# Keeping only the low part of a split weight in DRAM, and casting its high part again in the second pass

## The chip, the cores and the metric

The kernel runs on one core of one Trainium2 chip. The metric is the device time of one execution in microseconds (us). TensorE (PE in the profile; PEld is its weight load), VectorE (DVE), ScalarE (ACT), GpSimd (POOL) and SyncE (SP) each run their own list of instructions in order and wait for one another by semaphores. All DMAs of this kernel are issued from SP's list, one after the other; SPq in the profile is that issuing.

## The reference

One step of a hybrid decoder layer over 1024 prompt tokens and 8 single sample tokens, width 1024, all in float32:

```python
p = jnp.einsum('btd,dn->btn', x, w_in)                    # 1024 -> 9360 columns
p_gla, p_rwkv, p_gate = _split(p, (GLA_COLS, RWKV_COLS, GATE_COLS))
...  # gated linear attention: 4 heads, chunked, with a state
...  # RWKV-7: 16 heads, a recurrence over the tokens, with a state
m = (jax.nn.sigmoid(gate_a) * jnp.einsum('btc,cd->btd', o_gla, w_up_gla)
     + jax.nn.sigmoid(gate_b) * jnp.einsum('btc,cd->btd', o_rwkv, w_up_rwkv))
out = jnp.einsum('btd,de->bte', m, w_out)
y_out = _layernorm(DEEPNORM_ALPHA * x + out, ln_g, ln_b, LN_EPS)
```

The outputs are `y_out` for both groups of tokens and their new states.

## The kernel before

**Two passes over the tokens.** The tokens are split into two tiles: the first 512 prompt tokens and the 8 samples (520 columns, worked on as pieces of 256 and 264), and the other 512 prompt tokens (one piece of 512). For each tile the whole input projection is done, 73 blocks of 128 output columns, and between its matmuls the scans of that tile (GLA heads, RWKV pairs with a triangular solver) are woven in. Only then come, for both tiles, the two up projections (8 blocks each per tile, "the up stage"), the output projection and the layer norm ("the last stage").

**Split weights.** TensorE's float32r matmul rounds its operands, so each weight and each x is held as two parts: `hi`, the value cast to float32r, and `lo`, the rest. A block of the projection is 8 steps over the depth, and each step is three matmuls: hi times x high, hi times x low, lo times x high. A block's weight comes in two halves of 512 columns. A half is loaded as `wraw` (128 x 512 float32, 256 KB, 3 buffers). ScalarE casts it into `wpart[:, 0]`, VectorE (or GpSimd) subtracts and writes `wpart[:, 1]` (128 x 2 x 512, 512 KB, 5 buffers). TensorE takes the halves in order from the list `self.ws`, and a `wpart` buffer is free again when its block's last piece is done.

**What the second pass does for its weights.** The weights of the two passes are the same. So in the first pass each finished half is also written to DRAM, both parts together (`kept`, a DRAM tile named `w<column>_<half>`, 512 KB), and in the second pass the half is loaded from there, both parts in one DMA, with no work on ScalarE or VectorE. The profile calls the write `w<-wpart` and the reload `wpart<-w`. This is `load_w`, with its streams `high` (the casts) and `low` (the subtractions and the writes). The up projections' weights come the first pass's way: load, cast, subtract.

**What sets the order.** Nothing is ordered by hand. Every piece of work is a generator (a stream), and `Order.run` holds all streams. At each turn it prices the next operation of each stream with its own table of costs and gaps, takes the one that can start earliest (less a priority of its kind), puts it at the end of its engine's list, and goes on. Any change of one operation can therefore change the order of everything behind it, on every engine. All instructions are recorded in helpers, so nearly all of them show line L219 in the profile: groups are told apart by tile names. Names that the text below uses: `proj`, `big`, `pch`, `pY` are PSUM banks (2, 4, 1, 1 of them); `xs` the split x; `row` general rows in SBUF; `wide`, `rh`, `bk`, `gg`, `XT`, `X`, `A`, `L`, `LD`, `XD` belong to the scans, and `XD`, `L`, `XT`, `X` to the solver, which sends its blocks through DRAM by 16 DMAs in a row (`XD<-X`, `L<-gg`, `XT<-XD`, `X<-XD`, four each).

`evacuate` empties the bank of a finished piece. `up_row` and `load_gates` merge the two branches in the up stage: the first branch's result goes to the DRAM tile `mg`, and `c.half` tells that it may be read back.

Of the kernel before, what the change touches and what calls it, by code (L numbers as in the profile page):

```python
# [10 lines left out]
F32 = mybir.dt.float32  # L11
# [9 lines left out]
P = 128  # L21
# [397 lines left out]
class Kern(Order):  # L419
# [224 lines left out]
    def load_w(self):  # L644

        H = NK // 2
        todo = [(b.src, b.c0, j, b.c.i) for b in self.plan if b.src is not None for j in range(2)]
        raws, his, los, kept = [], [], [], {}

        def high():  # L650
            n = 0
            while True:
                yield lambda: len(raws) > n
                w = yield from self.get("wpart")
                yield self.A.copy(w[:, 0], raws[n][0])
                his.append(w)
                n += 1
                if n == count:
                    return

        def low():
            for n in range(count):
                yield lambda: len(his) > n
                w = his[n]
                raw, src, c0, j, i = raws[n]
                yield self.E.tensor_sub(w[:, 1], raw, w[:, 0].bitcast(F32))
                self.free(raw)
                if src is self.a["w_in"] and i == 0:
                    kept[c0, j] = self.dr.tile([P, 2, 512], F32, name=f"w{c0}_{j}")
                    yield self.S.dma_start(kept[c0, j], w.bitcast(F32))  # L670
                self.ws.append(w)
                los.append(w)
            self.w_done = True
        count = sum(src is not self.a["w_in"] or i == 0 for src, _, _, i in todo)
        self.spawn(high(), "w")
        self.spawn(low(), "w")
        for n, (src, c0, j, i) in enumerate(todo):
            if src is self.a["w_in"] and i:
                yield lambda: len(los) == len(raws)
                w = yield from self.get("wpart")  # L680
                yield self.S.dma_start(w.bitcast(F32), kept[c0, j])
                self.ws.append(w)
                continue
            raw = yield from self.get("wraw")

            yield from self.load(f"w{n}", self.S.dma_start(raw, src[c0 // P, j]))
            raws.append((raw, src, c0, j, i))

    def blocks(self):
        xs = None  # L690
        for at, b in enumerate(self.plan):
            if b.swap is not None:
                self.spawn(self.load_x(*b.swap), "x")
            if xs is None:
                yield lambda: len(self.xq) > 0
                xs = self.xq.pop(0)
            if b.src is None:
                yield from b.act(xs)
                xs = None
# [4 lines left out]
            tiles = list(enumerate(b.c.tiles))  # L704
            for group in [tiles] if at == 0 else [[x] for x in tiles]:
                fin = group[-1][0] == len(tiles) - 1
                banks = []
                for _ in group:
                    banks.append((yield from (self.get("proj") if b.src is self.a["w_in"] else self.get_of("proj", "pY", "big"))))
                for k in range(NK):  # L710
                    yield lambda: len(xs) > k
                    if len(w) <= k // 4:
                        yield lambda: self.ws
                        w.append(self.ws.pop(0))
                    hi, lo = (w[k // 4][:, v, k % 4 * P:k % 4 * P + P] for v in range(2))
                    xh, xl = xs[k]
# [9 lines left out]
                self.spawn(self.evacuate(evac, group, banks, b.post if fin else None), "evacuate")  # L726
            if b.last:
                xs = None

    def evacuate(self, evac, group, banks, post):  # L730
        for (tt, (t0, n)), ps in zip(group, banks):
            yield from evac(tt, t0, n, ps[:, :n])
            self.free(ps)
        if post is not None:
            post()
# [742 lines left out]
    def load_gates(self):  # L1478

        yield lambda: self.projected  # L1480
        for c in self.ctx:
            for n in range(2):
                for x in range(NK):
                    gt = yield from self.row(c.n, SPARE_ROWS)
                    yield self.S.dma_start(gt, self.sg[c.i][n][x])
                    m = None
                    if n:
                        m = yield from self.row(c.n, SPARE_ROWS)
                        yield lambda: c.half > x
                        yield self.S.dma_start(m, self.mg[c.i][x])  # L1490
                    yield self.A.activation(gt, gt, AF.Sigmoid)
                    self.gts.append((gt, m))

    def up_row(self, c, n, x):
        turn = self.ups
        self.ups += 1
        yield lambda: len(self.gts) > turn

        def ev(tt, t0, w, q):
            gt, m = self.gts[turn]  # L1500
            s = slice(t0, t0 + w)
            yield self.V.tensor_mul(gt[:, s], q, gt[:, s])
            if n:
                yield self.E.tensor_add(gt[:, s], gt[:, s], m[:, s])
            if tt == len(c.tiles) - 1:
                yield self.S.dma_start(self.mg[c.i][x], gt)
                self.free(gt)
                c.half += 1
                if n:
                    self.free(m)  # L1510
                    c.merged += 1
        return ev
# [205 lines left out]
    def run_all(self):  # L1718
        self.chained, self.headed, self.decayed = -1, 0, 0
        self.first = ["wa", "x0", "w0", "x1", "x2", "x3", "w1", "x4", "x5", "x6", "x7", "pv", "shift", "w2", "w3", "cst"]  # L1720
        self.has = set()
        self.sampled = self.w_done = self.projected = False
        self.ups = 0
        self.plan, self.xq, self.ws, self.wo, self.gts, self.l2s = [], [], [], [], [], []
        self.setup()
        self.ctx = [SimpleNamespace(i=i, base=b, n=n, ns=ns, tiles=t, gla_done=0, rwkv_done=0, fronts=0, lw_ready=False,
                                    alr_ready=0, merged=0, half=0, gated=0,
                                    rg=[[] for _ in range(NPAIR)], gg=[[] for _ in range(GH)])
                    for i, (b, n, ns, t) in enumerate(PASS)]
# [67 lines left out]
```

## Time and profile before

| | us |
|---|---|
| median of 3 runs | 1497.9 (1496.89 to 1500.17) |
| the profiled execution | 1493.88 |
| its span, first to last instruction | 1492.1 |
| TensorE busy | 1466.4 |
| TensorE weight load busy | 1282.5 |
| VectorE busy | 1201.9 |
| ScalarE busy | 880.1 |
| GpSimd busy | 115.5 |

The profiled execution lies 4.0 us below the median of the timed runs, and 1.8 us of it are outside the span. The core moved 197.32 MB from HBM and 118.61 MB to it. The first pass takes the first 600 us of the span, about; the second pass goes to 1190, the up stage to about 1390, and the last stage to the end. Engine times in the profile are busy times of the engine; a busy TensorE counts pipelined matmuls whose ends are modelled, so its idle time alone does not tell how dense its work is.

### The profile page before, as it was taken

The numbers are of one execution on the slowest core, as the hardware profiler recorded it, in microseconds if no ns is written. First come the engines' busy times: TensorE is split into PE (matmuls) and PEld (weight loads), VectorE is DVE, ScalarE is ACT, GpSimd is POOL, SyncE is SP. The second block draws the span as 40 slices with busy tenths as digits, with TensorE's granted clock in tenths as the row PEclk, the third lists the DMA queues.
The fourth block names the chain that finished last, engine by engine and source line by source line (L and its number), as shares of the span: only waits on it lengthen the run. The fifth ranks groups of instructions, "written<-read, shape, count | busy, mean of one in ns | idle before, by whom it ended". The sixth has DMA issues, their size and how long they took to land.

```text
span 1492.1 us, 30560 instructions
## 1 busy us (share of the span) xinstructions
PE 1466.4 (98%) x10678; PEld 1282.5 (86%) x10678; DVE 1201.9 (81%) x3159; ACT 880.1 (59%) x2221; POOL 115.5 (8%) x217
## 2 busy tenths in 40 slices
PE   9999999999999999999999999999999999999997
PEld 6998999999999999787877887787788899988786
DVE  6697889988998898979887998888777876756665
ACT  6665767767677677565754556465646746644210
POOL 1001002101120002001001010101000000000000
PEclk9999999999999999999999999999999999999999
DMA  9876697668767877675566565656554768887432
GB/s 310 282 267 207 221 314 227 218 220 302 234 220 221 297 239 241 185 237 168 165 203 175 161 199 180 181 154 171 177 172 135 234 197 258 282 300 264 143 106 85
DMA packets 211253, 319.01 MB, mean 214 GB/s; under 512 B 91683, under 2 KB 107180, under 8 KB 211100
## 3 DMA queue, kind: packets, MB, share of 16 engines
q1 hardware_dynamic: 211100, 317.06, 66.6%
q8 instruction: 85, 1.39, 0.4%
q14 instruction: 68, 0.56, 0.1%
HBM read 197.32 MB, written 118.61 MB: 212 GB/s over the span
## 4 chain that ended last, share of the span: by engine, by line
PE 83%; DVE 7%; DMA 4%; ACT 2%; issue 1%; SPq 1%; POOL 0%; POOLq 0%; DVEq 0%; ACTq 0%
PE proj L219 51%; PE big L219 22%; PE pch L219 6%; PE pY L219 5%; DVE row L219 2%; SPq L219 1%; DMA row<-o_rwkv 1%; ACT row L219 1%; DMA wraw<-w_in 1%; DVE X L219 1%; DVE wpart L219 1%; DMA wide<-LD 1%; DMA row<-state_rwkv 1%; DVE Xt L219 0%; ACT L397 0%
## 5 line engine op out<-in xcount | busy, mean ns | idle before, releaser
L219 PE MATMUL proj<-xs,wpart 128*128 128x264 f32 (+2 forms) x5640 | 1028.6, 327 | 1.2 <-DVE row L219 0.8
L219 PEld LDWEIGHTS proj<-xs,wpart 128*128 128x128 f32 x5640 | 814.4, 189 | 80.8 <-issue 10.3
L219 ACT CAST wpart<-wraw 128x512 fp32r<-128x512 f32 x210 | 130.2, 623 | 84.1 <-PE big L219 31.0
L219 DVE TENSOR_TENSOR wpart<-wraw,wpart 128x512 fp32r<-128x512 f32 x205 | 142.5, 697 | 33.4 <-ACT wpart L219 30.2
L219 DVE TENSOR_TENSOR row<-row 128x512 f32<-128x512 f32 (+10 forms) x295 | 156.8, 536 | 10.9 <-DMA row<-state_rwkv 6.2
L219 ACT ACTIVATE row<-row 128x512 f32<-128x512 f32 (+4 forms) x229 | 138.6, 610 | 26.2 <-DVE row L219 13.8
L219 POOL TENSOR_TENSOR row<-row 128x256 f32<-128x256 f32 (+7 forms) x74 | 70.3, 955 | 669.5 <-DVE row L219 232.9
L219 DVE TENSOR_TENSOR Xt<-X,wide 128x60 f32<-128x60 f32 (+24 forms) x496 | 108.4, 218 | 15.4 <-DMA wide<-LD 2.7
L219 DVE TENSOR_TENSOR X<-X,Xt 128x60 f32<-128x60 f32 (+24 forms) x496 | 106.0, 214 | 12.0
L219 ACT ACTIVATE row<-proj,omu 128x256 f32<-128x256 f32 (+1 forms) x99 | 54.3, 549 | 72.2 <-PE proj L219 71.8
L219 PE MATMUL big<-xs,wpart 128*128 128x512 f32 (+2 forms) x552 | 93.5, 324 | 0.0
L219 PEld LDWEIGHTS big<-xs,wpart 128*128 128x128 f32 x552 | 81.1, 188 | 8.7
L219 PE MATMUL big<-row 128*128 128x128 f32 (+4 forms) x464 | 86.6, 317 | 0.3 <-DVE Xt L219 0.3
L397 ACT ACT_TABLE_LOAD x64 | 82.1, 1283 | 1.1
L219 DVE SCALAR_TENSOR_TENSOR wide<-pch,pc,s0p 64x64 f32<-64x64 f32 x208 | 58.5, 281 | 28.3 <-PE pch L219 23.9
L219 DVE SCALAR_TENSOR_TENSOR row<-proj,pv,row 128x255 f32<-128x255 f32 (+1 forms) x99 | 56.3, 569 | 30.2 <-ACT tail L219 23.0
L219 ACT COPY row<-wide 64x64 f32<-64x64 f32 x240 | 57.9, 241 | 32.7 <-DVE wide L219 25.2
L219 ACT COPY wide<-pch 64x64 f32<-64x64 f32 x165 | 34.2, 207 | 65.1 <-PE pch L219 63.7
L219 PEld LDWEIGHTS big<-row 128*128 128x128 f32 (+3 forms) x464 | 60.5, 175 | 8.2 <-ACT row L219 0.8
L219 ACT COPY row<-big 128x128 f32<-128x128 f32 (+7 forms) x140 | 39.9, 313 | 41.7 <-PE big L219 40.4
L219 ACT ACTIVATE row<-proj 128x128 f32<-128x128 f32 (+4 forms) x136 | 36.9, 324 | 31.2 <-PE proj L219 30.5
L219 PE MATMUL big<-part,headsr 128*128 128x512 f32 x128 | 53.4, 418 | 1.7 <-DVE part L219 1.7
(234 smaller groups left out, 2025.8 us busy)
## 6 DMA issues: line engine op xcount, KB each, us to landing
w<-wpart SPq DMA_DIRECT2D x146, 512.0 KB
wpart<-w SPq DMA_DIRECT2D x146, 512.0 KB
wraw<-w_in SPq DMA_DIRECT2D x146, 256.0 KB
wide<-LD SPq DMA_DIRECT2D x64, 128.0 KB
wraw<-w_up_gla SPq DMA_DIRECT2D x32, 256.0 KB
wraw<-w_up_rwkv SPq DMA_DIRECT2D x32, 256.0 KB
sg<-row SPq DMA_DIRECT2D x16, 260.0 KB
row<-sg SPq DMA_DIRECT2D x16, 260.0 KB
```

The source lines that it names most:

```text
L219: ways.append((eng, lambda call=call: call(out, *args, **kw), price(eng, name, out, args, ins)))
L397: self.nc.scalar.preload_act_table_set(self.table)
```

## The change

In the first pass only `wpart[:, 1]`, the low part, is written to DRAM: 256 KB for each of the 146 halves where 512 KB were written. In the second pass a half takes two DMAs of 256 KB: the low part from DRAM into `wpart[:, 1]`, and the raw weight from `w_in` into a `wraw` buffer, which the second pass did not use before. A new stream, `second`, casts it on ScalarE into `wpart[:, 0]` and frees `wraw`. Since a half is now finished by one of two streams, `give` sorts them back into the order of the blocks. Three smaller edits go with it: `evacuate` empties the pieces of one block in their order (`past`), and `c.half` becomes the set of rows whose first branch has been written instead of a count.

```diff
         todo = [(b.src, b.c0, j, b.c.i) for b in self.plan if b.src is not None for j in range(2)]
-        raws, his, los, kept = [], [], [], {}
+        raws, his, los, kept, again, split = [], [], [], {}, [], {}
+
+        def give(n, w):
+            split[n] = w
+            while given[0] in split:
+                self.ws.append(split.pop(given[0]))
+                given[0] += 1
+        given = [0]
...
+        def second():
+            for n in range(len(todo) - count):
+                yield lambda: len(again) > n
+                at, w, raw = again[n]
+                yield self.A.copy(w[:, 0], raw)
+                self.free(raw)
+                give(at, w)
 
         def low():
...
                 if src is self.a["w_in"] and i == 0:
-                    kept[c0, j] = self.dr.tile([P, 2, 512], F32, name=f"w{c0}_{j}")
-                    yield self.S.dma_start(kept[c0, j], w.bitcast(F32))
-                self.ws.append(w)
+                    kept[c0, j] = self.dr.tile([P, 512], F32, name=f"w{c0}_{j}")
+                    yield self.S.dma_start(kept[c0, j], w[:, 1].bitcast(F32))
+                give(at, w)
                 los.append(w)
...
+        self.spawn(second(), "w")
         for n, (src, c0, j, i) in enumerate(todo):
             if src is self.a["w_in"] and i:
                 yield lambda: len(los) == len(raws)
                 w = yield from self.get("wpart")
-                yield self.S.dma_start(w.bitcast(F32), kept[c0, j])
-                self.ws.append(w)
+                yield self.S.dma_start(w[:, 1].bitcast(F32), kept[c0, j])
+                raw = yield from self.get("wraw")
+                yield self.S.dma_start(raw, src[c0 // P, j])
+                again.append((n, w, raw))
                 continue
...
-    def evacuate(self, evac, group, banks, post):
+    def evacuate(self, evac, group, banks, post, past):
         for (tt, (t0, n)), ps in zip(group, banks):
+            yield lambda: len(past) == tt
             yield from evac(tt, t0, n, ps[:, :n])
+            past.append(tt)
             self.free(ps)
...
-                        yield lambda: c.half > x
+                        yield lambda: x in c.half
...
-                c.half += 1
+                if not n:
+                    c.half.add(x)
```

How the lists change is shown at three places. The first is SP's list early in the first pass, with the loads of raw halves and the writes of finished ones (`w_1_...` is the DRAM tile of a half 1). Before:

```order
L219 DMA w_1_1102<-wpart 128x1024
L219 DMA wraw<-w_in 128x512
L219 DMA w_0_1142<-wpart 128x1024
L219 DMA wraw<-w_in 128x512
L219 DMA sg_93<-row 128x520
```

And after:

```order
L219 DMA w_1_1107<-wpart 128x512
L219 DMA wraw<-w_in 128x512
L219 DMA w_0_1145<-wpart 128x512
L219 DMA wraw<-w_in 128x512
L219 DMA sg_93<-row 128x520
```

The row of DMAs is the same; each write has 512 elements a partition instead of 1024.

The second place is SP's list in the second pass, at the solver of the fourth RWKV pair (its 16 DMAs through `XD`, `L`, `XT` and `X`). Before:

```order
L219 DMA wpart<-w_0_4875 128x1024
L219 DMA XD_13071<-X 256x1x32 x4
L219 DMA L_13089<-gg 32x4x32 x4
L219 DMA XT_168<-XD_13071 32x8x32 x4
L219 DMA X_173<-XD_13071 32x4x32 x4
L219 DMA wpart<-w_1_4929 128x1024
L219 DMA wpart<-w_0_4978 128x1024
L219 DMA wpart<-w_1_5105 128x1024
L219 DMA wpart<-w_0_5143 128x1024
```

And after:

```order
L219 DMA wpart<-w_0_5078 128x512
L219 DMA XD_13322<-X 256x1x32 x4
L219 DMA L_13360<-gg 32x4x32 x4
L219 DMA XT_168<-XD_13322 32x8x32 x4
L219 DMA X_173<-XD_13322 32x4x32 x4
L219 DMA wraw<-w_in 128x512
L219 DMA wpart<-w_1_5105 128x512
L219 DMA wraw<-w_in 128x512
L219 DMA wpart<-w_0_5158 128x512
L219 DMA wraw<-w_in 128x512
```

One half's reload has become two DMAs, and here the solver's 16 stand between them. In 129 of the 146 pairs the two follow each other at once, in 15 one to three rows stand between, and in two, this one and one early in the pass, a solver's 16 DMAs.

The third place is ScalarE's list at the same solver (`XT1`, `X20`: the solver's tiles; `big_13482`: the bank of its last product). Before, between the evacuation of one block (`proj_13109`) and that of the next (`proj_13193`):

```order
L219 COPY tail_161<-proj_13109 128x1
L219 COPY A_13211<-big_13189 128x128
L219 ACTIVATE row_13108<-carry_162,row_13108,pv_76 128x1
L219 COPY XT1_168<-big_13215 32x4x32 x4
L219 COPY gg_12334<-az_12333 64x8x64 x2
```

And after, from just ahead of the cast of that half to the evacuation of the next block:

```order
L219 ACTIVATE row_13354<-row_13351 128x8x64
L219 CAST wpart_13323<-wraw_13326 128x512
L219 ACTIVATE row_13351<-row_13351 128x512
L219 COPY XT1_168<-big_13482 32x4x32 x3
L219 CAST wpart_13437<-wraw_13446 128x512
L219 ACTIVATE row_13417<-proj_13418 128x256
```

Two casts now stand in this stretch, one ahead of the solver's copies and one ahead of the evacuation of a finished block; both wait for their raw load. Last, TensorE's list where it first uses that half (`wpart_13323`):

```order
L219 MATMUL proj_13418<-xs_9433,wpart_13291 128x512
L219 MATMUL big_13482<-X20_173,A_13479 32x128 x4
L219 MATMUL proj_13418<-xs_9432,wpart_13291 128x512
L219 MATMUL proj_13502<-xs_8879,wpart_13323 128x512
```

The half's first matmul is the second proj matmul behind the solver's product with `A`, where before six stood between that product and the half reloaded behind the solver:

```order
L219 MATMUL big_13215<-X20_173,A_13211 32x128 x4
L219 MATMUL proj_13193<-xs_9342,wpart_13049 128x512
L219 MATMUL proj_13193<-xs_9343,wpart_13049 128x512
L219 MATMUL proj_13193<-xs_9342,wpart_13049 128x512
L219 MATMUL proj_13193<-xs_9354,wpart_13049 128x512
L219 MATMUL proj_13193<-xs_9355,wpart_13049 128x512
L219 MATMUL proj_13193<-xs_9354,wpart_13049 128x512
L219 MATMUL proj_13193<-xs_9368,wpart_13079 128x512
```

Over the whole program ScalarE has 92 instructions more (146 casts come, 54 copies and casts have gone to VectorE), VectorE 48 more, GpSimd 6 more, and SP 146 DMAs more. TensorE has the same 9106 instructions in another order.

More of the change, by code (lines that the diff above doesn't have):

```diff
@@ L647, in load_w @@
         todo = [(b.src, b.c0, j, b.c.i) for b in self.plan if b.src is not None for j in range(2)]
-        raws, his, los, kept = [], [], [], {}
+        raws, his, los, kept, again, split = [], [], [], {}, [], {}
[5 more added lines that the diff above has]
+        given = [0]
         def high():
-            n = 0
-            while True:
+            for n in range(count):
                 yield lambda: len(raws) > n
@@ L656, in high @@
                 his.append(w)
-                n += 1
-                if n == count:
-                    return
+        def second():
[5 more added lines that the diff above has]
+                give(at, w)
         def low():
@@ L664, in low @@
                 w = his[n]
-                raw, src, c0, j, i = raws[n]
+                raw, src, c0, j, i, at = raws[n]
                 yield self.E.tensor_sub(w[:, 1], raw, w[:, 0].bitcast(F32))
@@ L686, in load_w @@
             yield from self.load(f"w{n}", self.S.dma_start(raw, src[c0 // P, j]))
-            raws.append((raw, src, c0, j, i))
+            raws.append((raw, src, c0, j, i, n))
     def blocks(self):
@@ L703, in blocks @@
             w = []
-            tiles = list(enumerate(b.c.tiles))
+            tiles, past = list(enumerate(b.c.tiles)), []
             for group in [tiles] if at == 0 else [[x] for x in tiles]:
@@ L725, in blocks @@
                         self.free(w[k // 4])
-                self.spawn(self.evacuate(evac, group, banks, b.post if fin else None), "evacuate")
+                self.spawn(self.evacuate(evac, group, banks, b.post if fin else None, past), "evacuate")
             if b.last:
                 xs = None
-    def evacuate(self, evac, group, banks, post):
+    def evacuate(self, evac, group, banks, post, past):
         for (tt, (t0, n)), ps in zip(group, banks):
+            yield lambda: len(past) == tt
             yield from evac(tt, t0, n, ps[:, :n])
+            past.append(tt)
             self.free(ps)
@@ L1726, in run_all @@
         self.ctx = [SimpleNamespace(i=i, base=b, n=n, ns=ns, tiles=t, gla_done=0, rwkv_done=0, fronts=0, lw_ready=False,
-                                    alr_ready=0, merged=0, half=0, gated=0,
+                                    alr_ready=0, merged=0, half=set(), gated=0,
                                     rg=[[] for _ in range(NPAIR)], gg=[[] for _ in range(GH)])
```

## The prediction

> **What bounds the kernel now.** I read the busy times and the chain that ended last first, then a table by stage, then TensorE's own waits, then what the two paths of a weight cost.
>
> ```profile
> PE 1466.4 (98%) x10678; PEld 1282.5 (86%) x10678; DVE 1201.9 (81%) x3159; ACT 880.1 (59%) x2221; POOL 115.5 (8%) x217
> PE 83%; DVE 7%; DMA 4%; ACT 2%; issue 1%; SPq 1%; POOL 0%; POOLq 0%; DVEq 0%; ACTq 0%
> ```
>
> TensorE (PE) is busy 98% of the span and carries 83% of the chain. The stages, with the columns PE, weight load, VectorE, ScalarE and GpSimd busy, granted clock, DMA share and GB/s; the last row is a stretch with nothing but 512-wide matmuls:
>
> ```profile
> 0.00:600.00 600.00, 591.17 (x5224) 558.18 (x5225) 514.17 (x1388) 417.88 (x1128) 61.63 (x124) 1.00 0.76 251
> 600.00:1190.00 590.00, 583.24 (x3662) 472.35 (x3661) 492.44 (x1388) 346.61 (x853) 50.74 (x89) 1.00 0.60 181
> 1250.00:1300.00 50.00, 50.00 (x456) 49.31 (x456) 35.66 (x80) 29.75 (x64) 0.00 (x0) 1.00 0.78 256
> 1300.00:1350.00 50.00, 50.00 (x217) 40.46 (x216) 30.01 (x47) 25.88 (x45) 0.00 (x0) 1.00 0.91 311
> ```
>
> The granted clock is full in both passes, and PE idles 8.8 us in the first and 6.8 us in the second. Is a busy PE also dense? In the last row 217 matmuls fill 50 us, one per 0.23 us, and the weight load shows 81%. The second pass shows 80% (472 of 590), so it is about as dense. What PE waits for, over the whole program (total us, times, longest us):
>
> ```profile
> PE pch L219 <- DVE wide L219: 4.4, 6, 1.8
> PE pch L219 <- DVE rh L219: 2.5, 4, 1.0
> PE big L219 <- DMA X<-XD: 1.8, 1, 1.8
> PE big L219 <- POOL XT L558: 1.7, 1, 1.7
> PE big L219 <- DVE part L219: 1.7, 1, 1.7
> PE big L219 <- DVE X L219: 1.5, 3, 0.6
> ...
> PE pch L219 <- DMA wide<-Sp: 0.7, 1, 0.7
> ...
> PE big L219 <- ACT row L219: 0.3, 1, 0.3
> ...
> PE proj L219 <- ACT wpart L219: 0.2, 1, 0.2
> ...
> PE pch L219 <- ACT row L219: 0.2, 1, 0.2
> PE proj L219 <- DVE wpart L219: 0.2, 1, 0.2
> ```
>
> All sixteen rows of this view come to 17 us. The weights are in it with 0.2 us for a cast and 0.2 us for a subtraction, and no reload at all. So the change touches a path that is almost wholly covered: it can give back little, and the question is whether it uncovers something.
>
> **The change part by part.** The sum is made against the profiled execution, 1493.9 us, which lies 4.0 us under the median of 1497.9; I carry the sum over to the median.
>
> *The first pass writes less.* What the queue moved, its share of 16 engines' time, and the transfers of weights:
>
> ```profile
> q1 hardware_dynamic: 211100, 317.06, 66.6%
> w<-wpart SPq DMA_DIRECT2D x146, 512.0 KB
> wpart<-w SPq DMA_DIRECT2D x146, 512.0 KB
> ```
>
> 146 writes lose 256 KB each, 38.3 MB. The queue takes 66.6% of 1492 us for 317 MB, 3.13 us a MB, so 120 us of DMA time leave the first pass: its share goes from 0.76 to about 0.56, and writes to HBM fall from 118.6 to 80.3 MB. What can it give? Only the PE waits that end on a DMA or right behind one: `X<-XD` 1.8, `DVE X` 1.5 (the solver's next step) and `wide<-Sp` 0.7, together 4.0 us. I take -1.5, with ends 0 and -4: shorter queues shorten these DMAs but don't remove their issue from one list.
>
> *The second pass reads as much as before* (two times 256 KB for 512 KB), so its DMA share stays at 0.60.
>
> *ScalarE casts 146 halves more.* Casts by stage (same columns, weight tiles only), then the form, then ScalarE's waits: one row of the first pass, one of the second.
>
> ```profile
> 0.00:600.00 600.00, 490.93 (x3512) 446.58 (x3512) 98.69 (x141) 90.81 (x146) 6.61 (x5) 1.00 0.76 251
> 600.00:1190.00 590.00, 478.48 (x1771) 315.78 (x1770) 1.98 (x3) 2.97 (x5) 0.00 (x0) 1.00 0.60 181
> ```
>
> ```profile
> L219 ACT CAST wpart<-wraw 128x512 fp32r<-128x512 f32 x210 | 130.2, 623 | 84.1 <-PE big L219 31.0 <-PE proj L219 30.3 <-PE pY L219 6.4
> ```
>
> ```profile
> ACT wpart L219 <- DMA wraw<-w_in: 4.1, 6, 1.1
> ```
>
> ```profile
> ACT wide L219 <- PE pch L219: 51.5, 42, 3.2
> ```
>
> 146 x 0.623 = 91 us on ScalarE, which goes from 347 to at most 438 of 590 us, 74%. The cover is the first pass itself: there ScalarE is 70% and VectorE 86% busy (418 and 514 of 600) with the same 146 casts, and PE idles 1.5%. VectorE takes 48 operations more by the lists; even at the 0.697 us of the subtraction that is 33 us, from 492 to at most 525 of 590, 89%, and its copies are shorter than that. I take 0 for it, with ends -2 and +3 (the waits on `wide`, `rh`, `part`, 8.6 us in all, shift a little either way with any new order).
>
> *Casts that wait for their load.* In the first pass a raw load goes ahead as soon as a raw buffer is free, long before its cast, and only 6 of 146 casts waited, 0.7 us each. In the second pass the two loads go out only once a `wpart` buffer is free, and the cast comes behind them. What is queued behind a waiting cast: copies of `pch` for the scans and evacuations of `proj`; TensorE waits for both. What speaks for little harm is that ScalarE itself waits for PE there (42 waits of 1.2 us on `pch`): it is mostly early, and a late cast eats that time first. If half the casts wait 0.7 us, ScalarE loses 51 us, of which I take 1 us on PE's path, since PE's waits on ScalarE are now 0.7 us in sixteen rows; the ends are 0 and +10 (a fifth of 51).
>
> *The reload behind the solver.* This is the place where PE itself may wait. Before, SP's list, PE's, and four transfers of the chain (start, duration):
>
> ```profile
> 913.99 1.88 SPq L219 DMA_DIRECT2D X<-XD  x4
> 915.97 1.80 SPq L219 DMA_DIRECT2D wpart<-w  x4
> ```
>
> ```profile
> 919.38 0.42 PE L219 MATMUL big<-X,A 128*32 128x128 f32 x8
> 919.74 1.89 PE L219 MATMUL proj<-xs,wpart 128*128 128x512 f32 x7
> ```
>
> ```profile
> 262.52 4.93 DMA wraw<-w_in
> ...
> 267.53 0.62 ACT wpart L219
> ```
>
> ```profile
> 485.11 3.78 DMA wraw<-w_in
> ```
>
> ```profile
> 1063.11 4.38 DMA wpart<-w
> ```
>
> Six matmuls of 0.23 us behind 919.7 the reloaded half was used, at 921.1, 5.2 us after its issue, and it needs about 4.4: covered by 0.8. After, the raw load has that slot in SP's list, but the half is used as the second proj matmul behind the product with `A`: at 919.7 + 0.23 = 919.9, 4.0 us after the issue. It needs 3.8 to 4.9 us for the load and 0.62 for the cast, 4.4 to 5.5: PE waits 0.4 to 1.5 us, I take 1. Three more halves stand nearly as close in the new lists; for them together I take 1, with ends 0 and 3.
>
> The Trainium skill speaks against this part of the change: its page "DMA: Bandwidth & Descriptors", in the section "Anatomy of one DMA", gives a DMA some 2.0 us fixed and 436 KB a us on top, measured on another issuing path. Cutting 512 KB into two of 256 KB halves only the small part: by it 3.2 us become two of 2.6. The trace agrees that size hardly counts (256 KB in 3.8 and 4.9 us, 512 KB in 4.4), but both take longer than the page has them. By the page's 2.6 us the cast would end before the 4.0 are over, the places would cost 0 and the sum be 2 us lower.
>
> *SP and PE's lists.* SP issues 146 DMAs more in a pass where it mostly waits:
>
> ```profile
> SPq L219 <- PE proj L219: 215.7, 95, 6.9
> ```
>
> At the 0.45 us of the rows above that is 66 us of list, against these 216 us of waiting for buffers to come free. PE has the same instructions; its rows of equal ones go from 2012 to 2022, and ten more changes of kind at 0.2 us are 2 us at most either way: 0. The order of evacuations and `c.half` move nothing that PE waited for: 0.
>
> The sum: -1.5 + 0 + 1 + 1 + 1 + 0 = +1.5 us, 1495.4 by the profile and 1499.4 by the median. All the ends together give -4 - 2 + 0 + 0.4 + 0 - 2 = -7.6 and 0 + 3 + 10 + 1.5 + 3 + 2 = +19.5.
>
> **The rivals.** *Slower: the casts hold up ScalarE's list.* One mechanism: the raw load lands after the cast's turn, ScalarE stands, and copies of `pch` behind it come late to a scan for which PE's list leaves no room. For it: the pair of loads is tied to the release of `wpart`, and PE's largest waits are already on `pch` (6.9 of 17 us). Against it: 3 halves are loaded ahead, ScalarE is early by 1.2 us at those copies. It decides once most casts wait longer than that; with the +10 above and the two terms for PE's own waits the sum is -1.5 + 10 + 2 = +10.5, about 1508. Chance 0.30.
>
> *Faster: the lighter first pass reaches PE.* The solver's round trips through DRAM get shorter and the second pass stays covered: -4 and a lucky order of VectorE's work, -2: 1492. For it: the wait on `X<-XD`, 1.8 us long. Against: nothing else of PE's waits hangs on bandwidth. Chance 0.19.
>
> *Faster by more: PE is not the bound.* If a weight load at 93% in the first pass (558 of 600) means that PE pauses between matmuls because it is fed late, a lighter DMA would close the pauses up to the 98.6% of the stretch from 1250 to 1300 (49.31 of 50): 600 x (0.986 - 0.93) = 34 us, 1464. Against it: the first pass has narrow solver and scan matmuls between, and the waits on weights are 0.4 us. The page "Perfetto Trace Analysis" of the Trainium skill, in its section "Identifying the Most-Contended Engine", has it that busy matmul time says little and that the weight load's share is the measure, which here is 86%. The 80% and 81% of the two rows above, one of them a stretch without a gap, show that this share is low for wide matmuls without any pause. Chance 0.03.
>
> **How the numbers follow.** The rest, 0.48, is the forecast: the path stays covered and a few microseconds go each way. A change under 0.2% (3 us) can't be told from none for this kernel. The forecast's cases lie between -3 and +6, three quarters of them within 3 us and a quarter above; so same is 0.38, slower 0.30 + 0.10 = 0.40, faster 0.22. The range: from 1491 (the lower rival's sum, with a bit to spare) to 1511 (3 us above the upper rival); it leaves out the rest of the upper ends and the case of 1464, about 2 in 10. The forecast's own range is 1495 to 1504.
>
> **What the profile after would show.** HBM writes of 80 MB and a DMA share near 0.56 in the first pass: the relief is real. About 150 casts in the second pass at 0.62 us and ScalarE at 70 to 74% of it. The sum of casts waiting for `wraw<-w_in`: under 60 us, and PE's waits for ScalarE below 3 us, if the cover holds; well above, the first rival is true. A PE wait of about 1 us on a cast at the fourth solver of the second pass. PE's waits on `X<-XD` gone or smaller. I am wrong if PE's idle time in the second pass goes beyond 15 us, or if the first pass shortens by more than 4 us.

## The result and the profile after

The changed kernel takes 1505.07 us (median, 1504.39 to 1506.58) against 1497.85 of the kernel before, timed beside it: a ratio of 1.0055, 95% interval 1.0040 to 1.0071. Timed once more with the later runs it gave 1.0069 (1.0054 to 1.0084). It is slower by 0.55 to 0.7%, some 7 to 10 us. The time lies within the predicted range of 1491 to 1511, but 5.7 us above the sum of 1499.4 and 1.1 above the forecast's own range of 1495 to 1504. Slower had the largest chance by a little (0.40, against 0.38 for the same); it came, but not by the way for which it was given.

The profiled execution took 1504.76 us with a span of 1503.0. First the line of busy times of the kernel after, and its two passes (columns PE, weight load, VectorE, ScalarE, GpSimd busy with counts, granted clock, DMA share, GB/s):

```profile
PE 1471.3 (98%) x10678; PEld 1282.5 (85%) x10678; DVE 1214.0 (81%) x3207; ACT 944.1 (63%) x2313; POOL 126.3 (8%) x223
```

```profile
0.00:600.00 600.00, 589.11 (x5183) 555.41 (x5184) 507.38 (x1385) 411.53 (x1107) 65.61 (x124) 1.00 0.62 185
600.00:1190.00 590.00, 581.43 (x3653) 467.75 (x3652) 501.29 (x1418) 407.23 (x951) 56.25 (x94) 1.00 0.59 179
```

The relief is there: the first pass's DMA share fell from 0.76 to 0.62. So are the casts: ScalarE's busy time in the second pass rose from 347 to 407 us of 590. What to see beside them is the count of matmuls in the first row: by 600 us TensorE has done 5183 where the kernel before had done 5224. In the pass that got lighter it is 41 matmuls late. A better mark of the end of the first pass is the first 512-wide matmul of `proj`, with which the second pass begins: it is row 4505 of TensorE's list before and row 4512 after. From the timelines (start, duration), before and after:

```profile
597.26 0.48 PE L219 MATMUL proj<-xs,wpart 128*128 128x512 f32 x1
```

```profile
604.34 1.40 PE L219 MATMUL proj<-xs,wpart 128*128 128x512 f32 x5
```

The first pass ends 7.1 us later. Of these, 1.9 us arise in the first 14 us of the trace and are not the change (the last section shows why), so some 5 us are left. Over the span, TensorE's idle time went from 1492.1 - 1466.4 = 25.7 to 1503.0 - 1471.3 = 31.7 us, so 6.0 of the 10.9 us between the two spans are idle; the rest is longer busy time for the same 10678 instructions. What TensorE waits for, largest first (total us, times, longest us):

```profile
PE pch L219 <- DVE wide L219: 8.5, 13, 1.7
PE big L219 <- DVE part L219: 2.8, 4, 1.0
PE pch L219 <- DVE rh L219: 2.4, 4, 1.1
...
PE pch L219 <- ACT wide L219: 1.5, 2, 1.2
...
PE big L219 <- DMA X<-XD: 1.1, 1, 1.1
...
PE big L219 <- ACT row L219: 0.6, 1, 0.6
...
PE pch L219 <- ACT row L219: 0.3, 1, 0.3
PE proj L219 <- ACT wpart L219: 0.3, 1, 0.3
```

The wait on `wide`, tiles that VectorE writes for the scans, has nearly doubled (4.4 before), and all rows on VectorE come to 17.2 us (12.6 before). A cast of a weight still costs 0.3 us, and all rows on ScalarE together 2.7. By this view most of the loss isn't where the casts are.

### The profile page after: what moved, and what is told of

Same layout as the page of the kernel before. It is cut to its first block, busy times and chain, and to the rows that moved or that the text cites. A ratio compares the mean times of both kernels' runs of the same rounds, so it can differ in the third digit from the quotient of the medians.

```text
span 1503.0 us, 30956 instructions
## 1 busy us (share of the span) xinstructions
PE 1471.3 (98%) x10678; PEld 1282.5 (85%) x10678; DVE 1214.0 (81%) x3207; ACT 944.1 (63%) x2313; POOL 126.3 (8%) x223
## 3 DMA queue, kind: packets, MB, share of 16 engines
q1 hardware_dynamic: 232124, 278.79, 60.7%
HBM read 197.32 MB, written 80.34 MB: 185 GB/s over the span
## 4 chain that ended last, share of the span: by engine, by line
PE 80%; DVE 9%; DMA 5%; ACT 3%; issue 2%; SPq 1%; POOL 0%; POOLq 0%; DVEq 0%; ACTq 0%
PE proj L219 49%; PE big L219 21%; PE pch L219 5%; PE pY L219 4%; DVE row L219 3%; DMA wraw<-w_in 2%; ACT row L219 1%; SPq L219 1%; DVE X L219 1%; DVE wide L219 1%; DVE wpart L219 1%; DVE part L219 1%; DMA row<-o_rwkv 1%; DMA wide<-LD 1%; DVE Xt L219 1%
## 5 line engine op out<-in xcount | busy, mean ns | idle before, releaser
L219 ACT CAST wpart<-wraw 128x512 fp32r<-128x512 f32 x356 | 219.3, 620 | 118.7 <-PE proj L219 34.9
L219 DVE TENSOR_TENSOR row<-row 128x256 f32<-128x256 f32 (+6 forms) x285 | 151.9, 539 | 4.1 <-DMA row<-state_rwkv 0.8
L219 ACT ACTIVATE row<-row 128x512 f32<-128x512 f32 (+4 forms) x229 | 138.0, 610 | 25.3 <-DVE row L219 15.4
L219 POOL TENSOR_TENSOR row<-row 128x512 f32<-128x512 f32 (+7 forms) x84 | 79.0, 946 | 766.7 <-DVE row L219 334.2
L219 PE MATMUL big<-xs,wpart 128*128 128x512 f32 (+2 forms) x576 | 100.9, 327 | 0.1
L219 PEld LDWEIGHTS big<-xs,wpart 128*128 128x128 f32 x576 | 85.9, 188 | 10.4 <-DVE xs L219 0.5
L219 ACT COPY row<-wide 64x64 f32<-64x64 f32 x240 | 57.8, 241 | 18.8 <-DVE wide L219 14.2
L219 ACT COPY row<-big 128x384 f32<-128x384 f32 (+6 forms) x144 | 41.9, 308 | 42.6 <-PE big L219 41.1
L219 PE MATMUL pch<-wide,gg 128*128 128x128 f32 x256 | 51.7, 283 | 6.4 <-DVE wide L219 4.7
L219 PEld LDWEIGHTS pch<-wide,gg 128*128 128x128 f32 x256 | 42.0, 188 | 17.0 <-PE proj L219 5.5
```

Of the source, the lines that this page charges most:

```text
L219: ways.append((eng, lambda call=call: call(out, *args, **kw), price(eng, name, out, args, ins)))
```

## The experiments

Three theories were set against each other. A: the casts and the two loads of a half cost time in the second pass. B: the scheduler prices a write of 256 KB lower than one of 512 KB, this rewrites every engine's list from the first pass on, and the new lists are worse. C: that is nothing special to this change, any rewriting of the lists moves this kernel by some microseconds. All ratios are to the kernel before on the same chip, with 95% intervals.

**Price the write as before.** The changed kernel, with the scheduler told the old cost of a 512 KB write. The chip still writes 256 KB, but the first pass's lists are as before: TensorE's is the same for 4411 of the some 4500 rows ahead of the second pass.

```diff
-                    yield self.S.dma_start(kept[c0, j], w[:, 1].bitcast(F32))
+                    op = self.S.dma_start(kept[c0, j], w[:, 1].bitcast(F32))
+                    op.lag = (P * (0.01 + 4096 * 4.65e-5) / 16, 1.2)
+                    yield op
```

> The changed kernel, but its scheduler is told that the write of a low part takes the queue as long as the old 512 KB write did. So the lists of the first pass stand as they did before the change, while the chip writes 256 KB; the second pass has the low reload, the raw load and the cast, as changed. Theory A (the casts and split reloads of the second pass cost the time): 1503 to 1507. Theory B (the time is lost in the first pass, whose lists were written anew because the scheduler priced the writes lower): 1495 to 1499. Theory C (any rewritten order moves this kernel by some microseconds either way, whatever the cause): anywhere from 1490 to 1508.

Measured: 1498.95 us, ratio 1.0014 (1.0001 to 1.0026). Its first pass, the start of its second, and its casts' waits there (ScalarE's waits between 574 and 1200 us):

```profile
0.00:600.00 600.00, 591.04 (x5218) 557.45 (x5219) 515.04 (x1386) 419.13 (x1130) 60.27 (x124) 1.00 0.62 187
```

```profile
598.02 0.71 PE L219 MATMUL proj<-xs,wpart 128*128 128x512 f32 x2
```

```profile
ACT wpart L219 <- DMA wraw<-w_in: 34.2, 30, 2.5
```

One number in the scheduler's table brings back most of the loss. TensorE has done 5218 matmuls by 600 us, nearly the 5224 of before, and its second pass begins at 598.0 (597.3 before), with the same light writes as after (share 0.62). The casts wait longer here than in the kernel after, where it is 25.2 us.

```profile
ACT wpart L219 <- DMA wraw<-w_in: 25.2, 29, 2.6
```

So the kernel with the longer waits is the faster one, which speaks against A.

**Write both parts, read one.** The lists of the experiment above, row for row, but 512 KB are written.

```diff
-                    kept[c0, j] = self.dr.tile([P, 512], F32, name=f"w{c0}_{j}")
-                    yield self.S.dma_start(kept[c0, j], w[:, 1].bitcast(F32))
+                    kept[c0, j] = self.dr.tile([P, 2, 512], F32, name=f"w{c0}_{j}")
+                    yield self.S.dma_start(kept[c0, j], w.bitcast(F32))
...
-                yield self.S.dma_start(w[:, 1].bitcast(F32), kept[c0, j])
+                yield self.S.dma_start(w[:, 1].bitcast(F32), kept[c0, j][:, 1])
```

> The changed kernel, but the first pass writes both parts again (512 KB), as before the change; the second pass reads the low one alone, loads the raw weight and casts it. Every list but for the size of these writes is that of the run with the old price. Against that run it shows the lighter writes alone: theory of the prediction: 1.5 us slower than it (0 to 4). Against before it shows the second pass alone: theory A 1503 to 1507, theory B 1497 to 1500.

Measured: 1500.36 us, ratio 1.0027 (1.0015 to 1.0040). First pass:

```profile
0.00:600.00 600.00, 591.73 (x5217) 558.66 (x5218) 513.61 (x1386) 419.35 (x1129) 60.81 (x124) 1.00 0.76 251
```

The DMA share is back at 0.76, the matmuls done are the same but for one, and the time is 1.4 us above the experiment before (1500.36 - 1498.95). That is what the lighter writes are worth: about 0.1%, and since the two intervals overlap, it is hardly told from nothing.

**No casts at all.** The changed kernel with its own prices; the second pass neither loads nor casts the raw half, a second DMA of the low part fills the high half instead.

```diff
-                raw = yield from self.get("wraw")
-                yield self.S.dma_start(raw, src[c0 // P, j])
-                again.append((n, w, raw))
+                yield self.S.dma_start(w[:, 0].bitcast(F32), kept[c0, j])
+                give(n, w)
```

> The changed kernel without the raw load and the cast in the second pass: the high part is filled by a second DMA of the same 256 KB low part, so the output is not the reference's. First pass as in the changed kernel, word for word. Theory A: the loss goes, 1496 to 1499. Theory B: it stays, 1503 to 1507.

Measured: 1506.22 us, ratio 1.0070 (1.0051 to 1.0089).

```profile
0.00:600.00 600.00, 590.15 (x5197) 556.31 (x5198) 509.27 (x1392) 411.86 (x1111) 64.80 (x122) 1.00 0.62 184
600.00:1190.00 590.00, 582.60 (x3654) 469.11 (x3653) 499.64 (x1390) 336.25 (x833) 58.47 (x98) 1.00 0.60 181
```

ScalarE is back at 336 us in the second pass, and the loss is as large as with the casts. A fails here, with the reserve that the scheduler also wrote other lists for the second pass.

**The same lists with and without casts.** To remove that reserve: the lists of the first experiment held as they are, the casts priced and ordered but not issued, and in the raw load's place in SP's list a DMA of the low part into the high half.

```diff
-                yield self.A.copy(w[:, 0], raw)
+                op = self.A.copy(w[:, 0], raw)
+                op.ways = [("A", lambda: None, op.ways[0][2])]
+                yield op
...
-                yield self.S.dma_start(raw, src[c0 // P, j])
+                op = self.S.dma_start(raw, src[c0 // P, j])
+                op.ways = [("S", lambda w=w, at=(c0, j): self.nc.sync.dma_start(w[:, 0].bitcast(F32), kept[at]), op.ways[0][2])]
+                yield op
```

> The run with the old price of the writes, every list kept as it is there, but without the 146 casts and raw loads of the second pass: the scheduler still prices them, the cast is left out, and the raw load's place in SP's list is taken by a DMA of the low part into the high half (the output is not the reference's). So the casts and their waits are taken away with no new order. If the casts and their waiting cost the time of the second pass: 2 to 4 us faster than the run with the old price, back to before less the lighter writes (about -0.1% on before). If they are covered: within 1.5 us of it.

Measured: 1498.01 us, ratio 1.0012 (1.0001 to 1.0023), against 1.0014 with the casts. The second pass with the casts (the run with the old price) and without them:

```profile
600.00:1190.00 590.00, 581.28 (x3628) 466.38 (x3628) 501.83 (x1412) 404.86 (x944) 53.77 (x91) 1.00 0.59 179
```

```profile
600.00:1190.00 590.00, 580.82 (x3626) 467.00 (x3626) 503.65 (x1413) 331.15 (x803) 56.24 (x91) 1.00 0.59 180
```

TensorE's, VectorE's and GpSimd's lists are the same row for row. ScalarE does 331 us of work here against 405 with the casts, and nothing follows from it: the two ratios differ by 0.0002, and with both intervals some 0.17% (2.5 us) either way is left for the casts and their waits together.

**Load the raw half first.** The first experiment's prices, with the raw load issued ahead of waiting for a `wpart` buffer, as in the first pass; then the same edit on the changed kernel with its own prices.

```diff
+                raw = yield from self.get("wraw")
+                yield self.S.dma_start(raw, src[c0 // P, j])
                 w = yield from self.get("wpart")
                 yield self.S.dma_start(w[:, 1].bitcast(F32), kept[c0, j])
-                raw = yield from self.get("wraw")
-                yield self.S.dma_start(raw, src[c0 // P, j])
                 again.append((n, w, raw))
```

With the old price:

> The run with the old price of the writes, with the two loads of the second pass in the other order: the raw load goes out as soon as a raw buffer is free, ahead of the wait for a weight buffer, and the low part follows. ScalarE's wait for raw loads should go (under 8 us for 25), and the place behind the solver with it. If these waits cost: 1495 to 1498. If not: within 3 us of the run with the old price.

Measured: 1496.50 us, ratio 1.0001 (0.9989 to 1.0013). ScalarE's waits in the second pass:

```profile
ACT wpart L219 <- DMA wraw<-w_in: 1.5, 2, 1.2
```

With the new price:

> The changed kernel itself (writes at their new price) with the raw load ahead of the low reload in the second pass. First pass as in the changed kernel. Theory B and C: the first pass's loss stays, 1501 to 1506. If the gain of the raw-first run over the run with the old price was the casts' waits and not its order, the same 2 us come off the changed kernel.

Measured: 1500.35 us, ratio 1.0033 (1.0020 to 1.0046). The casts' waits are gone in both (1.5 us, 2 times; 1.7 us, 4 times), yet the two differ by 0.32%, through the price alone. The first is the best version of the change, and it ties with the kernel before. The 0.13% by which it beats the first experiment may be the waits or may be the order; the pair with the same lists above found no cost of the waits.

Against the changed kernel (1506.07 on the same chip) the second is 5.7 us faster, where 2 us had been expected if the waits cost, and it lies just under the expected 1501 to 1506. This speaks for theory A, and no run with the same lists decides it. Against A stands the run with no casts at all, which has no such waits either and is as slow as the changed kernel (1.0070). So whether the 5.7 us are the waits or the new order of the second pass is not shown. The first pass's loss did stay, as expected: the second pass begins at 603.4 us.

**Price the raw load later.** The first experiment, with the scheduler told that the raw load lands 1 us later, so that it places the casts later.

```diff
+                op = self.S.dma_start(raw, src[c0 // P, j])
+                op.lag = (op.lag[0], op.lag[1] + 1.0)
+                yield op
```

> The run with the old price of the writes, in which the scheduler is also told that the second pass's raw loads land 1 us later, so that their casts stand further back in ScalarE's list. First pass as there. If casts that wait for their load cost time in the second pass: 1 to 3 us faster than the run with the old price, 1496 to 1498, with ScalarE's wait for the raw loads down from some 25 us to under 10. If they cost nothing: the same as it within 3 us either way, from the new order alone.

Measured: 1502.14 us, ratio 1.0043 (1.0026 to 1.0059).

```profile
ACT wpart L219 <- DMA wraw<-w_in: 12.8, 11, 2.5
```

The waits fell from 34.2 to 12.8 us, not quite to the 10 expected, and the kernel became 3.2 us slower, a little beyond the 3 us given for "the same". The waits of the casts don't order the times.

**Rewrite the lists for no reason.** For theory C the kernel before itself was given other lists, by three small changes of the scheduler's constants, one at a time; what the kernel computes, loads and writes stays as it was. One of the three was also made on the changed kernel, and the changed kernel was timed again.

```diff
-LANDED = 0.5
+LANDED = 0.6
```

> The kernel before, with one number of the scheduler changed that says nothing of this change: the margin that it leaves for a landed DMA, 0.6 us for 0.5. All lists are written anew, with the same instructions. Theories A and B say nothing on it; if the order alone is neutral, 1495 to 1501. Theory C: 3 to 10 us off the kernel before, either way.

Measured: 1504.48 us, ratio 1.0061 (1.0042 to 1.0079).

```diff
-BIAS = 0.1
+BIAS = 0.12
```

> The kernel before with another unrelated number of the scheduler changed (the handicap of VectorE in a choice between ScalarE and VectorE, 0.12 us for 0.1). Theory C, sharpened after the first four runs: the order of the kernel before is a lucky one, and nearly every rewritten order is slower, by 3 to 10 us: 1500 to 1507. If orders scatter evenly round it: 1490 to 1505, as likely below 1497 as above.

Measured: 1513.15 us, ratio 1.0117 (1.0097 to 1.0138), 6 us beyond the expected 1507.

```diff
-SPARE = 0.4
+SPARE = 0.45
```

> The kernel before with a third unrelated number of the scheduler changed (its margin for TensorE, 0.45 us for 0.4). Theory C: 1500 to 1513, slower than before as the two others were. If it lies under 1497, the order of the kernel before is not exceptional.

Measured: 1508.83 us, ratio 1.0086 (1.0073 to 1.0099). The changed kernel with `BIAS = 0.12`:

> The changed kernel with the same unrelated number changed. If the changed kernel's lost time is a matter of its order in general, another order of it lies at 1499 to 1508, within the scatter of the rewritten orders of the kernel before. If the changed kernel's own mechanism (lighter writes seen by the scheduler) costs, it stays at 1503 to 1507, and below 1500 would say that its order was an unlucky one.

Measured: 1506.38 us, ratio 1.0072 (1.0052 to 1.0091). Both of its cases allow this time, so it decides nothing between them. And the changed kernel again:

> The changed kernel again, on this chip, to set the other runs against it: 0.4 to 0.7% slower than before.

Measured: 1506.07 us, ratio 1.0069 (1.0054 to 1.0084).

Three of three reshuffles of the kernel before cost 0.6 to 1.2%, as much as the whole change or more. The worst of them shows the same signature, from the two profiled views (busy times; TensorE's waits):

```profile
PE 1477.1 (97%) x10678; PEld 1284.9 (85%) x10678; DVE 1213.3 (80%) x3180; ACT 873.3 (58%) x2207; POOL 108.8 (7%) x206
```

```profile
PE pch L219 <- DVE wide L219: 7.0, 9, 2.0
PE big L219 <- DVE part L219: 6.9, 8, 2.1
PE pch L219 <- DVE rh L219: 4.3, 7, 1.1
PE big L219 <- DVE X L219: 3.2, 5, 0.9
```

TensorE idles 1515.1 - 1477.1 = 38.0 us, and the growth is again in waits on VectorE's scan tiles, `wide`, `part`, `rh` and `X`, with no weight among them.

A part of the reshuffles' loss goes with a lower granted clock. The executions of `BIAS`, `LANDED` and `SPARE` have mean clocks of 0.9945, 0.9955 and 0.9968, against 0.9974 of the kernel before on the three chips. In the trace of `BIAS` the clock falls at three places, each time where TensorE stands idle for some 3 us of ten. One of them (TensorE's busy time first, the clock third from the end):

```profile
1240.00:1250.00 10.00, 7.03 (x53) 6.37 (x51) 4.34 (x10) 7.04 (x15) 0.00 (x0) 0.94 0.84 274
1250.00:1260.00 10.00, 9.47 (x60) 9.50 (x61) 3.82 (x11) 4.04 (x12) 0.00 (x0) 0.72 0.53 168
```

What it is worth can be estimated from the kernel before: its 14 executions at 0.999 average 1495.1 us, its 7 at 0.994 or 0.995 average 1499.6, about 1 us for each 0.001 of clock. By this estimate some 3, 2 and 0.6 us of the 17, 8 and 12 us of the three go with the clock, and some 2 of the 3.2 us that pricing the raw load later cost (0.9963 against 0.9985 with the old price alone). The clock takes no part in the change's own loss: the changed kernel ran at means of 0.9985 and 0.9978, and with the old price at 0.9985.

Over all kernels, from their profiled spans (the ratio is of all executions, the other columns of the profiled one):

| kernel | ratio | PE busy, us | PE idle, us | PE waits on VectorE, us |
|---|---|---|---|---|
| before | 1 | 1466.4 | 25.7 | 12.6 |
| old price, raw half first | 1.0001 | 1468.9 | 25.2 | 11.1 |
| old price, no casts, same lists | 1.0012 | 1468.7 | 26.4 | 15.1 |
| old price | 1.0014 | 1470.6 | 26.9 | 15.4 |
| old price, both parts written | 1.0027 | 1469.4 | 27.1 | 11.9 |
| after, raw half first | 1.0033 | 1471.5 | 28.3 | 13.5 |
| old price, raw load priced later | 1.0043 | 1473.4 | 28.8 | 13.8 |
| after | 1.0055, 1.0069 | 1471.3, 1473.0 | 31.7, 33.1 | 17.2, 18.8 |
| before, `LANDED` | 1.0061 | 1475.2 | 31.7 | 16.6 |
| after, no casts | 1.0070 | 1473.7 | 30.6 | 14.7 |
| after, `BIAS` | 1.0072 | 1473.0 | 32.3 | 18.3 |
| before, `SPARE` | 1.0086 | 1471.9 | 34.6 | 22.3 |
| before, `BIAS` | 1.0117 | 1477.1 | 38.0 | 23.2 |

Idle time of TensorE rises with the time nearly throughout, whether a row has the casts, the light writes, both or neither. The column of waits goes along roughly.

## Why the prediction was right and wrong

**The path of a weight stays covered: right, as far as the runs show.** ScalarE came to 407 of 590 us, 69% (70 to 74 forecast, at most 438 us). The casts waited 25.2 us (under 60 forecast), TensorE for ScalarE 2.7 us (under 3), and VectorE came to 501 of 590 (at most 525 forecast). TensorE's idle time in the second pass stayed at 590 - 581.4 = 8.6 us (below the 15 that would have refuted it). The pair with the same lists puts the casts' own cost at nothing that can be told from zero, where the sum had +1.

**The first pass writes less: right for the time, as far as 1.4 us can be told, wrong in the DMA time.** HBM writes fell to 80.34 MB, and the wait on `X<-XD` from 1.8 to 1.1 us, though other orders move it as much (1.8 with the light writes and the raw load priced later). The term was -1.5; writing the other 256 KB again cost 1.4. The DMA share is 0.62, not 0.56: the relief is 0.14 x 600 = 84 us and not 120. The price was wrong: 120 us came from the mean of the whole queue, 3.13 us a MB, but the 38.3 MB that went had taken only 84 / 38.3 = 2.2. The pair that differs in these bytes alone says the same. The queue (packets, MB, share) and the memory with the light writes, from the page after, and the queue of the run with the old price and of the run that writes both parts:

```profile
q1 hardware_dynamic: 232124, 278.79, 60.7%
...
HBM read 197.32 MB, written 80.34 MB: 185 GB/s over the span
```

```profile
q1 hardware_dynamic: 232124, 278.79, 60.5%
```

```profile
q1 hardware_dynamic: 232124, 317.07, 65.9%
```

In as many packets the 38.3 MB take 65.9% of 1496.5 less 60.5% of 1497.5 us, 80 us or 2.1 us a MB. A mean over a queue isn't the price of its large writes. What is left is dearer by the MB: 60.7% of 1503 us for 278.8 MB is 3.27.

**The reload behind the fourth solver: wrong in size, +1 that was 0.** SP's list, the cast, and TensorE's use, from the timeline of the kernel after (start, duration):

```profile
926.69 0.38 SPq L219 DMA_DIRECT2D wraw<-w_in  x1
...
929.56 0.62 ACT L219 CAST wpart<-wraw 128x512 fp32r<-128x512 f32 x1 [0.28 <-DMA wraw<-w_in]
...
931.49 0.42 PE L219 MATMUL big<-X,A 128*32 128x128 f32 x8
...
931.85 1.43 PE L219 MATMUL proj<-xs,wpart 128*128 128x512 f32 x5
```

The cast waited for its load until 929.56, so the load took 2.87 us from its issue, not 3.8 to 4.9. Half and cast were there at 930.18, and TensorE came to the next product only at 931.49. Here the Trainium skill's page "DMA: Bandwidth & Descriptors", in its section "Anatomy of one DMA", was nearer with its 2.6 us than the rows that I took, although those rows were loads of the same size in the same kernel. How busy the DMA engines were doesn't explain it: their share was 0.46 around the load of 4.93 us (262 to 268 us), 0.83 around that of 3.78 (485 to 489), and 0.67 here (924 to 932). What made those two longer isn't shown. The page's way of reckoning, "the places would cost 0", came true.

**The order of the lists: the step that failed.** The sum took 0 for VectorE's waits in a new order, with ends of -2 and +3, and 0 for SP's and PE's lists, with 2 either way. Together they measure 7 us: the changed kernel's 1.0055 and 1.0069 against 1.0014 with the old price, from nothing but lists. The first pass, whose shortening by more than 4 us would have refuted the prediction, became some 5 us longer instead: the second pass begins between 597.3 and 599.3 us in the six traces with the old lists of the first pass, and between 603.4 and 604.3 in the four with the new ones. With the slow start taken out, the four are 5 to 6 us behind the kernel before. I had priced the operations in the lists and taken the rest for noise around zero. It is not centred on zero: of the three reshuffles of the kernel before, all are slower, by 0.6 to 1.2%, and no version of the change beats it. Why before's order is better than these others isn't shown; it may be that its constants had been chosen by the time of that very order, but no run here tests it.

**The slower rival had the time and not the cause: luck.** It gave 1508 by casts that hold up ScalarE, and the kernel came within 3 us of that. The upper end of the range, 1511, came from this rival too; the forecast's own range ended at 1504. Without the experiments the nearness to 1508 would have passed for its proof. The loss stays without any cast (1.0070), and goes with a price that leaves the casts where they are (1.0014). The rivals of 1492 and 1464 didn't come: a lighter first pass gives TensorE 1.4 us, and the weight load stays at 93% of the first pass (555 of 600), so there were no pauses that a lighter DMA closed.

**What stays open.** Which rows of the rewritten lists cost the 7 us: some 5 us are lost by the end of the first pass, but the lists differ in thousands of places, and no single one was tried. Nor is it settled what gave the 5.7 us that loading the raw half first took off the changed kernel, and whether the 0.12 to 0.14% that is left with the old price, with and without casts, is the second pass's own new order; the version that loads the raw half first doesn't have it, and that is another order too.

## What to carry to other kernels

Where a scheduler orders the work, a change of one operation is two changes, the operation and a new order: hold the order (here by leaving the old price in the table) to measure the first, and reshuffle the old kernel a few times to see how large the second is before giving a difference under 1% a cause. In the prediction, such an order term belongs in the sum with the spread that reshuffles show, and with its sign open to the slower side where the old order may be the best of many. A load that doesn't need the scarce buffer goes ahead of the wait for that buffer: it took the casts' waits from 34 to 1.5 us, and neither kernel became slower by it (2.4 and 5.7 us faster, by the waits or by the new order).

## What the runs showed of the hardware that was not expected

**The start of TensorE's work varies by 2 us between executions.** Two kernels with the same rows there (old price, and old price with the raw half first), timeline of TensorE's first microseconds (start, duration), in this order:

```profile
5.69 1.60 PE L219 MATMUL proj<-xs,wpart 128*128 128x256 f32 x7 [0.18 <-ACT wpart L219]
7.22 1.24 PE L219 MATMUL big<-row,wa 128*16 128x256 f32 x16
8.39 3.13 PE L219 MATMUL proj<-xs,wpart 128*128 128x256 f32 x24
```

```profile
5.73 2.18 PE L219 MATMUL proj<-xs,wpart 128*128 128x256 f32 x7 [0.22 <-ACT wpart L219]
7.84 1.94 PE L219 MATMUL big<-row,wa 128*16 128x256 f32 x16
9.71 3.84 PE L219 MATMUL proj<-xs,wpart 128*128 128x256 f32 x24
13.47 1.07 PE L219 MATMUL big<-row,wa 128*16 128x256 f32 x16
```

The same sixteen matmuls take 1.24 or 1.94 us (1.07 for the next sixteen of their kind), and the second kernel is 2.0 us behind when its 24 matmuls end (11.5 against 13.5), though it is the faster of the two by its median. The Trainium skill's page "TensorE: Matmul & The Clock Gate", in the section "What's actually happening", tells of a first stretch of some 3.4 us at half clock whose end depends on a window that runs freely. The trace agrees with a slow stretch of changing length, but here it is longer, with slow matmuls still at 9.71 us, 8 us after TensorE's first at 1.73; and as the granted clock reads 1.00 over it, the trace doesn't show that the clock is the cause. The kernel before was profiled with the short one and the kernel after with the long one:

```profile
7.89 1.94 PE L219 MATMUL big<-row,wa 128*16 128x256 f32 x16
```

Its next 24 matmuls end at 13.5 us as well, against 11.5 in the kernel before. So about 2 of the 10.9 us between the two profiled spans, counted as busy time, are not the change. The medians, some 7 to 10 us apart, are the measure; a comparison of two single traces at this size has to take such a stretch out first.
